# A decoder layer on one core: x and the first weights on one queue, cross attention in whole banks, w_co in turns with the heads, the last k-tiles of down block by block

## The chip, the core and the metric

The kernel runs on one core of a Trainium2 chip. The metric is device time in microseconds, from several executions; lower is better. One execution was also taken by the hardware profiler.

## What is computed

One decoder layer on a sequence of 256 tokens with a model width of 1024, in fp32, with 256 memory tokens for cross attention and a feed-forward width of 2816:

```python
x = x + 0.5 * swiglu(rms_norm(x, g_ffn1), w_ffn1_gu, w_ffn1_down)
h = rms_norm(x, g_mix); proj = h @ w_in            # q, k, v of 16 heads
x = x + concat(rms_norm(dilated attention, 12 heads), rms_norm(MoBA attention, 4 heads)) @ w_out
x = x + cross_attention(rms_norm(x, g_cross), rms_norm(mem, g_mem), w_cq, w_ckv, w_co)   # 4 heads of 256
x = x + 0.5 * swiglu(rms_norm(x, g_ffn2), w_ffn2_gu, w_ffn2_down)
return rms_norm(x, g_final)
```

Cross attention: q = h @ w_cq; k and v from mem @ w_ckv; scores times 1/16, softmax over the 256 memory tokens, times v, then @ w_co.

## The kernel before

Activations are kept transposed: `X[0..7]` are eight blocks of 128 features x 256 tokens. Every fp32 operand is split in two float32r parts, a high part and the rest (the low part), and a product is the sum of three: high x high, low x high, high x low. Weights are split by `wsplit` (ACT copies the high part, DVE subtracts for the low part: L125 and L126), activations by `split` (L313 and L314 without a gain, L316 and L317 with one). A split activation block lies as 256 columns of high and 256 columns of low part side by side.

Two ways to do the three products stand next to each other. `mmT_run` and `mm2` take one matmul with the high weights on all 512 columns and one with the low weights on the 256 high ones; the result is two halves of a 512-column PSUM bank, which `halves` or `add_halves` must add (an ACT copy, a DVE add) before anything else. `mm3` and `mmT_wide` take three matmuls of 256 columns into 256 columns of a bank; nothing has to be added. `mmT_wide` goes through all blocks with one operand before it takes the next. Each matmul has its weight load.

Weights come as chunks of 512 KB (two k-tiles x 512 columns) through four raw buffers, issued by SP (`wload`, L118), and are split into eight `w` buffers. `projT` is a projection of four blocks: `spread` takes all blocks k-tile by k-tile, `abreast` two blocks at a time, and the last `whole` blocks go as three products each. `downT` (first FFN only) and `addT` (w_out, w_co) add their result to X, and `block` then splits X for the next stage and adds its squares to the sum for the norm.

The order on TensorE is the program's; the other engines' order is set by the framework's planner, except in `start()`, where everything is in program order. To mix stages on TensorE the program keeps a clock by hand: every matmul helper calls `tick` with its estimated time, `later(d, f)` puts f on a list for d us on, and `tick` fires what is due. `until` fires events until something exists.

`start()` is the opening: x (1 MB in three pieces, by ACT's queue) and the first four weight chunks `w0(0)` to `w0(3)` (by SP's queue) are loaded, x is transposed by TensorE (`prepare(j)`, two blocks at a time), and the first gate projection runs k-tile by k-tile over four blocks with `mmT_wide` (L238). `WARM` = 5 matmuls on the identity run at the very start, two more between the first transposes and the first product (an fp32 matmul is two passes in the trace, so ten and four).

The cross stage: `cross_qp` makes q in two halves c (four blocks, two heads each); after each half its heads' `scores` are due by `later`, and each head's probabilities are transposed by `turn`, 5.0 behind its scores. `projT` emits all four blocks before the loop over them begins. `cross_o` makes a head's output from V and the transposed probabilities. In the w_co step, `addT` first takes k = 0 to 3 for all blocks, then calls `cross_o` for heads 2 and 3, then finishes block by block.

The mem load is in two halves (`half`), each transposed by `turn` some us behind on the hand-kept clock.

## Time and profile before

| | |
|---|---|
| time, median of 3 executions | 621.33 us (619.17 to 621.79) |
| profiled execution | 621.25 us |
| its span, first to last instruction | 619.5 us |
| TensorE busy | 601.9 us (97%) |
| VectorE (DVE) busy | 445.0 us (72%) |
| ScalarE (ACT) busy | 350.7 us (57%) |
| moved by DMA | 110.02 MB, mean 178 GB/s |

Busy time of TensorE is that of its matmuls, which are pipelined: a matmul's row lasts longer than the distance to the next one, so its speed is read from the spacing of starts. An idle time stands in brackets behind a row, with what ended it. PEld is the weight loads, L12 is line 12 of the program. The rows of the trace stand further down.

### The profile page before, as it was taken

Reading aid. Unit: us, or ns where it says so; the run is one execution under the profiler, and the core shown is the slowest. Engines: PE = TensorE matmul, PEld = TensorE weight load, DVE = VectorE, ACT = ScalarE, POOL = GpSimd, SP = SyncE. Lnnn points to the kernel's source line nnn. Section 1 sums busy time; section 2 is a strip of 40 time slices with the busy share of each in tenths; the row PEclk is TensorE's granted clock in tenths of the full one; section 3 lists DMA queues with packets and bytes.
Section 4 is the critical chain, followed back from the end, with each engine's and each line's share of the span. In section 5 each row is a group of like instructions: output and inputs, shape, how many; then the busy total and the mean of one; then the engine's idle time right before and its main releaser. Section 6 shows DMA issues by size and latency. Waiting matters only on the chain.

```text
span 619.5 us, 9485 instructions
## 1 busy us (share of the span) xinstructions
PE 601.9 (97%) x3488; PEld 519.4 (84%) x3488; DVE 445.0 (72%) x754; ACT 350.7 (57%) x614; POOL 57.0 (9%) x90
## 2 busy tenths in 40 slices
PE   7999999999999999999999998889999999999995
PEld 6998888888898887778878887778888888888885
DVE  3899747897475866774888886868788788794424
ACT  4766535665454665565675565756564565664312
POOL 0000110000010241222301120003000000000000
PEclk9999999999999999999999998999999999999999
DMA  7667997577666627444336644333646646476501
GB/s 238 227 213 245 208 243 231 181 236 252 213 188 191 199 88 237 137 137 137 122 116 204 234 138 140 105 99 112 230 149 224 204 153 222 170 242 201 167 1 68
DMA packets 58989, 110.02 MB, mean 178 GB/s; under 512 B 3760, under 2 KB 14608, under 8 KB 58944
## 3 DMA queue, kind: packets, MB, share of 16 engines
q1 hardware_dynamic: 56848, 104.44, 52.1%
q0 software_dynamic: 832, 2.88, 2.7%
q10 hardware_dynamic: 1264, 2.10, 0.9%
q8 instruction: 27, 0.44, 0.3%
q14 instruction: 18, 0.15, 0.1%
HBM read 107.58 MB, written 1.84 MB: 177 GB/s over the span
## 4 chain that ended last, share of the span: by engine, by line
PE 90%; DVE 4%; DMA 2%; ACT 2%; issue 1%; POOL 0%; ACTq 0%; POOLq 0%; SPq 0%
PE bank L224 41%; PE bank L228 20%; PE bank L188 7%; PE bank L189 7%; PE bank L190 7%; PE bank L238 3%; DVE w L126 2%; PE bank L490 1%; PE bank L537 1%; DMA slot<-in_x_dram 1%; PE bank L521 1%; DVE slot L317 1%; DMA slot<-in_mem_dram 1%; ACT w L125 1%; DMA raw<-in_w_co_dram 1%
## 5 line engine op out<-in xcount | busy, mean ns | idle before, releaser
L224 PE MATMUL bank<-slot,w 128*128 128x512 f32 x1162 | 364.4, 397 | 4.6 <-DVE slot L314 3.6
L126 DVE TENSOR_TENSOR w<-raw,w 128x1024 fp32r<-128x1024 f32 (+1 forms) x197 | 237.5, 1222 | 72.9 <-ACT w L125 72.3
L125 ACT ACTIVATE w<-raw 128x1024 fp32r<-128x1024 f32 (+1 forms) x197 | 201.9, 1051 | 96.1 <-PE bank L190 42.7
L228 PEld LDWEIGHTS bank<-slot,w 128*128 128x128 f32 x1162 | 214.6, 188 | 49.2 <-issue 1.5
L228 PE MATMUL bank<-slot,w 128*128 128x256 f32 x1162 | 228.2, 280 | 0.0
L224 PEld LDWEIGHTS bank<-slot,w 128*128 128x128 f32 x1162 | 180.0, 189 | 9.3 <-DVE slot L314 4.2
L270 ACT ACTIVATE hv<-bank 128x256 f32<-128x256 f32 x120 | 43.9, 376 | 36.0 <-PE bank L228 30.6
L188 PE MATMUL bank<-w,slot 128*128 128x512 f32 (+1 forms) x156 | 60.8, 390 | 0.0
L189 PE MATMUL bank<-w,slot 128*128 128x512 f32 (+1 forms) x156 | 60.0, 384 | 0.0
L190 PE MATMUL bank<-w,slot 128*128 128x512 f32 (+1 forms) x156 | 59.9, 384 | 0.0
L188 PEld LDWEIGHTS bank<-w,slot 128*128 128x128 f32 x156 | 29.3, 188 | 6.0 <-issue 0.5
L190 PEld LDWEIGHTS bank<-w,slot 128*128 128x128 f32 x156 | 29.3, 188 | 5.9
L189 PEld LDWEIGHTS bank<-w,slot 128*128 128x128 f32 x156 | 29.3, 188 | 5.5
L313 ACT ACTIVATE slot<-u 128x512 fp32r<-128x512 f32 x22 | 13.9, 630 | 31.6 <-DVE u L408 31.4
L335 POOL TENSOR_TENSOR ssq<-ssq,sq 128x256 f32<-128x256 f32 x28 | 24.3, 867 | 71.9 <-ACT sq L330 71.5
L317 DVE SCALAR_TENSOR_TENSOR slot<-X,gT,slot 128x256 fp32r<-128x256 f32 x30 | 19.9, 674 | 6.6 <-ACT slot L316 6.4
L271 DVE TENSOR_TENSOR u<-bank,hv 128x256 f32<-128x256 f32 x40 | 16.8, 421 | 9.7 <-ACT hv L270 9.6
L403 ACT ACTIVATE g<-g 128x512 f32<-128x512 f32 x22 | 13.7, 630 | 17.7 <-DVE g L285 17.7
L508 ACT ACTIVATE pt<-pt,nm 128x128 f32<-128x128 f32 (+1 forms) x32 | 14.2, 445 | 15.2 <-DVE nm L506 15.2
L271 DVE TENSOR_TENSOR g<-bank,hv 128x256 f32<-128x256 f32 x40 | 16.4, 421 | 8.6 <-ACT hv L270 8.4
L316 ACT ACTIVATE slot<-X,gT 128x256 fp32r<-128x256 f32 x30 | 14.8, 506 | 12.7 <-DVE X L296 12.7
L335 POOL TENSOR_TENSOR ssq<-sq 128x256 f32<-128x256 f32 x6 | 5.7, 945 | 172.6 <-ACT sq L330 172.6
(132 smaller groups left out, 523.1 us busy)
## 6 DMA issues: line engine op xcount, KB each, us to landing
raw<-in_w_ffn_gu_dram SPq DMA_DIRECT2D x88, 512.0 KB, 4.6
raw<-in_w_ffn_down_dram SPq DMA_DIRECT2D x44, 512.0 KB, 4.5
raw<-in_w_ckv_dram SPq DMA_DIRECT2D x16, 512.0 KB, 5.0
raw<-in_w_in_dram SPq DMA_DIRECT2D x12, 512.0 KB, 3.6
raw<-in_w_in_dram SPq DMA_DIRECT2D x24, 256.0 KB, 4.2
raw<-in_w_out_dram SPq DMA_DIRECT2D x8, 512.0 KB, 4.9
raw<-in_w_cq_dram SPq DMA_DIRECT2D x8, 512.0 KB, 5.1
raw<-in_w_co_dram SPq DMA_DIRECT2D x8, 512.0 KB, 3.8
```

The lines of the kernel that those rows point to most:

```text
L125: nc.scalar.activation(w[:, 0, a:b], raw[:, a:b], AF.Copy)
L126: nc.vector.tensor_tensor(w[:, 1, a:b], raw[:, a:b], w[:, 0, a:b].bitcast(F32), OP.subtract)
L188: nc.tensor.matmul(ps, ah, bh, start=start, stop=False)
L189: nc.tensor.matmul(ps, al, bh, start=False, stop=False)
L190: nc.tensor.matmul(ps, ah, bl, start=False, stop=stop)
L224: nc.tensor.matmul(ps, w[:, 0, o + blk * P:o + (blk + 1) * P], both(xs, k), start=k == first, stop=False)
L228: nc.tensor.matmul(ps[:, :256], w[:, 1, o + blk * P:o + (blk + 1) * P], both(xs, k)[:, :256], start=False, stop=k == last)
L238: nc.tensor.matmul(ps, w[:, wp_, o + blk * P:o + (blk + 1) * P], a, start=start and i == 0, stop=stop and i == 2)
L270: nc.scalar.activation(t, ps[:, 256:], AF.Copy)
L271: nc.vector.tensor_tensor(out, ps[:, :256], t, OP.add)
L317: nc.vector.scalar_tensor_tensor(l, src, g, h.bitcast(F32), OP.mult, OP.subtract)
L335: (eng or nc.gpsimd).tensor_tensor(new, self.ss, sq, OP.add)
```

## The change

Five places change. In `start()`, SP issues x too, in turns with w0: x's first 256 columns, w0(0), x's next 256, w0(1), x's last 512, w0(2), w0(3); and four instead of two identity matmuls run before the first product. In `downT` the last six k-tiles, instead of the last two, go block by block. The mem transposes are due 6.0 instead of 4.0 behind their load. In the cross stage, the first half of q goes through `mmT_wide` into 256 columns per block, the scores' delays change, and `cross_o` does one head per call with `mm3`, both parts in one bank. In w_co the steps alternate with heads 2 and 3: k = 0 for all blocks, k = 2 for two, head 2, k = 2 for the other two, head 3, then k = 4 and k = 6 for all.

```diff
     def load_x(c0, n):
         hf, o = divmod(c0, 512)
-        nc.scalar.dma_start(x0[hf].rearrange("p (a n) -> p a n", n=512)[:, :, o:o + n],
+        nc.sync.dma_start(x0[hf].rearrange("p (a n) -> p a n", n=512)[:, :, o:o + n],
                           x_in[0, :, c0:c0 + n].rearrange("(a p) n -> p a n", p=P))
...
     def projT(wk, xs, nblk, spread=False, whole=0, abreast=False):
         res = [bank() for _ in range(nblk)] if spread or abreast else []
+        if spread and whole:
+            res = [b[:, :256] for b in res]
+            for k in range(KT):
+                mmT_wide(res, wk, xs, k, k == 0, k == KT - 1)
+            return res
         if spread:
...
-            for k in range(0, FK - 2, 2):
+            for k in range(0, FK - 6, 2):
                 for blk in range(4):
                     step(k, blk)
             for blk in range(4):
-                step(FK - 2, blk)
+                for k in range(FK - 6, FK, 2):
+                    step(k, blk)
                 add_halves(X[c * 4 + blk], b[blk], 0.5)
                 block(c * 4 + blk)
 
-    def addT(wd, src, block, early=0, more=None):
+    def addT(wd, src, block, order=None):
         for c in range(2):
             wk = colchunk(wd, c * 512, 512)
-            if c == 0 and early:
+            if c == 0 and order:
                 b = [bank() for _ in range(4)]
-                for k in range(0, early, 2):
-                    for blk in range(4):
+                for step in order:
+                    if callable(step):
+                        step()
+                        continue
+                    k, blks = step
+                    for blk in blks:
                         mmT_run([(b[blk], k, blk), (b[blk], k + 1, blk)], wk, src, 0, KT - 1)
-                more()
-                for blk in range(4):
-                    for k in range(early, KT, 2):
-                        mmT_run([(b[blk], k, blk), (b[blk], k + 1, blk)], wk, src, 0, KT - 1)
-                    add_halves(X[blk], b[blk], 1.0)
-                    block(blk)
+                        if k == KT - 2:
+                            add_halves(X[blk], b[blk], 1.0)
+                            block(blk)
                 continue
...
-            later(4.0, turn, hf, m)
+            later(6.0, turn, hf, m)
...
-            for blk, ps in enumerate(projT(colchunk(w_cq, c * 512, 512), xs, 4, spread=(c == 0))):
+            for blk, ps in enumerate(projT(colchunk(w_cq, c * 512, 512), xs, 4, spread=(c == 0), whole=4 * (c == 0))):
...
-                    later(2.6 + 2.0 * (blk // 2) if c == 0 else 1.8, scores, c * 2 + blk // 2)
+                    later(3.0 + 3.0 * (blk // 2) * (c == 0), scores, c * 2 + blk // 2)
...
-    def cross_o(V, PT, OT, hs):
-        for h in hs:
-            until(lambda: PT[h] is not None)
-            t = work.tile([P, 512], F32, tag="g1", name="on", bufs=3)
-            for e in range(2):
-                et = (h % 2) * 2 + e
-                op = bank()
-                for i in range(2):
-                    vs = V[i][h // 2]
-                    mm2(op, vs[:, et * P:(et + 1) * P], vs[:, 512 + et * P:512 + (et + 1) * P],
-                        both(PT, h * 2 + i), i == 0, i == 1)
-                halves(t[:, e * 256:e * 256 + 256], op)
-            s = slot()
-            split(s, 0, 2, t)
-            OT.append(s)
+    def cross_o(V, PT, OT, h):
+        until(lambda: PT[h] is not None)
+        op = bank()
+        for e in range(2):
+            et = (h % 2) * 2 + e
+            for i in range(2):
+                vs = V[i][h // 2]
+                ph, pl = act(PT, h * 2 + i)
+                mm3(op[:, e * 256:e * 256 + 256], vs[:, et * P:(et + 1) * P],
+                    vs[:, 512 + et * P:512 + (et + 1) * P], ph, pl, i == 0, i == 1)
+        s = slot()
+        split(s, 0, 2, op)
+        OT.append(s)
...
     def start():
+        load_x(0, 256)
         nc.scalar.dma_start(grow[0:8], g_ffn1.rearrange("l (k p) -> (l k) p", p=P))
-        load_x(0, 256)
+        load_w0(0)
         load_x(256, 256)
+        load_w0(1)
         load_x(512, 512)
-        for i in range(4):
-            load_w0(i)
+        load_w0(2)
+        load_w0(3)
...
-        for i in range(2):
+        for i in range(WARM - 1):
             nc.tensor.matmul(gps[:, :P], ident, ident, start=True, stop=True)
...
-        cross_o(V, PT, OT, (0, 1))
+        cross_o(V, PT, OT, 0)
+        cross_o(V, PT, OT, 1)
         xs, st, block = next_x("ffn2")
-        addT(w_co, OT, block, 4, lambda: cross_o(V, PT, OT, (2, 3)))
+        every = range(4)
+        addT(w_co, OT, block, ((0, every), (2, (0, 1)), lambda: cross_o(V, PT, OT, 2), (2, (2, 3)),
+                               lambda: cross_o(V, PT, OT, 3), (4, every), (6, every)))
```

## Rows read from the trace of the kernel before

**Rows 1.** The page's busy times: busy us (share of the span) x instructions.

```profile
PE 601.9 (97%) x3488; PEld 519.4 (84%) x3488; DVE 445.0 (72%) x754; ACT 350.7 (57%) x614; POOL 57.0 (9%) x90
```

**Rows 2.** TensorE's matmuls in order of time, those with a wait ahead of them: start us, length us, line and operation, output <- inputs, [idle before <- what ended it].

```profile
7.28 1.12 PE L728 MATMUL bank<-ident,slot 128*128 128x128 f32 x4 [3.23 <-DMA slot<-in_x_dram]
...
208.42 1.20 PE L224 MATMUL bank<-slot,w 128*128 128x512 f32 x4 [0.75 <-DVE slot L317]
...
219.72 1.06 PE L566 MATMUL bank<-ident,slot 128*128 128x128 f32 x8 [0.42 <-DMA slot<-in_mem_dram]
...
375.15 0.39 PE L188 MATMUL bank<-slot 128*128 128x256 f32 x1 [0.36 <-ACT slot L313]
...
376.41 0.39 PE L189 MATMUL bank<-slot 128*128 128x256 f32 x1 [0.88 <-DVE slot L314]
...
402.31 0.50 PE L224 MATMUL bank<-slot,w 128*128 128x512 f32 x1 [1.92 <-DVE slot L314]
...
410.75 0.72 PE L224 MATMUL bank<-slot,w 128*128 128x512 f32 x2 [1.72 <-DVE slot L314]
```

**Rows 3.** The opening: instructions in order of time, and three pieces of the chain of waits (start us, length us, what).

```profile
3.78 0.27 PE L720 MATMUL bank<-ident,grow 8*128 8x8 f32 x1
...
8.19 1.06 PE L747 MATMUL bank<-ident 128*128 128x128 f32 x4
...
15.50 0.60 PE L728 MATMUL bank<-ident,slot 128*128 128x128 f32 x4
15.86 3.13 PE L238 MATMUL bank<-slot,w 128*128 128x256 f32 x24
...
21.42 3.90 ACT L125 ACTIVATE w<-raw 128x1024 fp32r<-128x1024 f32 x4
...
9.25 2.73 PE bank L238 x12
11.98 0.80 PE bank L728 x4
```

**Rows 4.** Transfers in the opening: the load of x's first piece in the chain of waits (issue ended at the start given, length to landing); bytes by queue up to 4.3 us (q1 is SP's queue, q10 ACT's; packets, MB, share of 16 engines); and four stretches (us from start, length, busy time of each engine, granted clock, DMA share, GB/s).

```profile
1.37 5.87 DMA slot<-in_x_dram
...
q1 hardware_dynamic: 364, 0.71, 54.0%
q10 hardware_dynamic: 17, 0.01, 0.5%
...
0.00:3.20 3.20, 1.85 (x8) 1.85 (x9) 0.17 (x2) 0.18 (x1) 0.68 (x6) 1.00 0.37 87
3.20:4.60 1.40, 0.85 (x5) 0.53 (x3) 0.17 (x1) 1.30 (x2) 0.00 (x0) 1.00 1.04 391
4.60:6.70 2.10, 0.00 (x0) 0.00 (x0) 0.00 (x0) 0.00 (x0) 0.00 (x0) 1.00 1.03 366
6.70:11.20 4.50, 3.92 (x18) 3.83 (x19) 2.17 (x4) 3.19 (x7) 0.00 (x0) 1.00 0.97 347
```

**Rows 5.** The end of down, in order of time: the first matmuls of the q projection, its sixth step, and the split of the seventh block.

```profile
199.09 1.09 PE L224 MATMUL bank<-slot,w 128*128 128x512 f32 x4
...
206.10 1.09 PE L224 MATMUL bank<-slot,w 128*128 128x512 f32 x4
...
207.41 0.95 DVE L317 SCALAR_TENSOR_TENSOR slot<-X,gT,slot 128x256 fp32r<-128x256 f32 x1
```

**Rows 6.** The second mem load in the chain of waits.

```profile
215.29 4.29 DMA slot<-in_mem_dram
```

**Rows 7.** The first cross scores: DVE's instructions in order of time, two stretches (columns as in rows 4, the granted clock third from the end), and the page's granted clock in 40 slices of 15.5 us.

```profile
374.23 0.42 DVE L271 TENSOR_TENSOR hq<-bank,hv 128x256 f32<-128x256 f32 x1
...
374.81 1.21 DVE L126 TENSOR_TENSOR w<-raw,w 128x1024 fp32r<-128x1024 f32 x1
...
375.94 0.42 DVE L314 TENSOR_TENSOR slot<-hq,slot 128x256 fp32r<-128x256 f32 x1
...
374.60:377.70 3.10, 1.52 (x7) 0.72 (x5) 2.89 (x10) 1.87 (x6) 0.00 (x0) 1.00 0.93 320
377.70:381.20 3.50, 3.50 (x15) 3.31 (x16) 2.33 (x8) 1.75 (x6) 0.00 (x0) 0.52 0.36 133
...
PEclk9999999999999999999999998999999999999999
```

**Rows 8.** The w_co step in order of time: the split of head 1's output, head 2's transposes and their split.

```profile
401.57 0.68 DVE L314 TENSOR_TENSOR slot<-on,slot 128x512 fp32r<-128x512 f32 x1
...
402.65 0.60 PE L658 MATMUL bank<-ident,cpt 128*128 128x128 f32 x4
...
403.28 0.60 ACT L313 ACTIVATE slot<-bank 128x512 fp32r<-128x512 f32 x1 [1.80 <-PE bank L658]
...
403.92 0.69 DVE L314 TENSOR_TENSOR slot<-bank,slot 128x512 fp32r<-128x512 f32 x1 [0.52 <-ACT slot L313]
```

**Rows 9.** Weight loads by line (count | busy us, mean ns of one | idle), and the time from issue to landing of the weight transfers in the first 40 us.

```profile
L228 PEld LDWEIGHTS bank<-slot,w 128*128 128x128 f32 x1162 | 214.6, 188 | 49.2 <-issue 1.5
L238 PEld LDWEIGHTS bank<-slot,w 128*128 128x128 f32 x144 | 18.9, 203 | 0.2
...
DMA to landing us min/median/max: 3.8/5.2/9.4
```

## The prediction

> **What bounds the kernel now.** I read the page's shares first: TensorE is busy 97% of the span [rows 1]. So only two things move the time: matmul work added or removed, and the places where TensorE waits. The order of its instructions is the program's own, so I next listed, in order of time, every place where it waited [rows 2]: for x at 7.28 us, at the end of the first down projection (208.42), for mem (219.72), at the first cross scores (375.15, 376.41), and twice in the first half of w_co (402.31 and 410.75). Besides waits, TensorE runs slowly in two stretches. At 377.7 to 381.2 the granted clock is 0.52 where it is 1.00 just before, nearly all of it at 1.2 instead of 2.4 GHz, right behind the waits at 375 and 376; it is the only one of the 40 slices that the page shows under nine tenths [rows 7]. In the opening the column for the granted clock reads 1.00 throughout [rows 4], but the spacing tells the same two levels: twelve 256-column matmuls from 9.25 take 2.73 us (0.23 each), twenty-four from 15.86 take 3.13 with the last one's tail (about 0.122 each) [rows 3]. Everything else on TensorE is one stream without gaps, so a stall taken out early stays out, unless a later one takes it back.
>
> **Opening.** The first transposes start at 7.28, when x's first 256 columns have landed; they were issued at 1.37 on ACT's queue [rows 2, 4]. Up to 4.3 us that queue moved 0.01 MB while SP's, with the weights, moved 0.71 [rows 4]. After the change x's first piece (262 KB) is the first on SP's queue. All queues together moved 87 GB/s x 3.2 us = 278 KB by 3.2 us, then 391 GB/s [rows 4]; so the piece is through by about 3.2 and landed by about 3.8, or 4.3 if its shorter 1 KB runs move more slowly at the start. TensorE is busy until 4.05 (gain transpose, 3.78 + 0.27) [rows 3]. Transposes therefore begin at 4.1 instead of 7.28. By the same running sum w0(0) (786 KB in all) is through at 4.5, x's second piece at 5.2, w0(1) at 6.7, x's last at 8.2, w0(2) and w0(3) at 9.7 and 11.2. With half a microsecond allowed for landing each is there before it is due: w0(3), the latest, was split before ACT began on the up half at 21.42 [rows 3], so not before 16 now.
>
> From transposes to the first real matmul it took 0.91 us and four matmul passes of warming, 8.19 to 9.25. Now there are four warming matmuls, each two passes: eight passes at 0.265 = 2.12, 1.06 more. Matmuls followed the warming without a wait before, when it was shorter, so ACT's and DVE's splits are in time and the first matmul is at 4.1 + 0.91 + 2.12 = 7.15. The twelve matmuls of k = 0 cost 2.73 at the low spacing or 12 x 0.122 = 1.46 at the high one, and the four transposes behind them 0.80 or 0.36 [rows 3]. I take the high one: the engine now works from 1.35 on with hardly a pause, where before it stood still 3.23 us ahead of the transposes and the spacing fell while it worked on. So matmuls of k = 1 start at 7.15 + 1.46 + 0.36 = 9.0 instead of 12.78: 3.8 earlier. Bounds: still the low spacing, 2.1; high spacing already in the warming passes, 4.8. I take 3.5. The transfers behind it are paced by the splits that free the four raw buffers, which move along.
>
> A rule speaks against this part: the Trainium skill ("DMA: Bandwidth & Descriptors", section "Issuing engines are not separate DMA queues") has transfers from several engines interleave on the same 16 DMA engines and lets the choice of the issuer save only issue time. Rows 4 disagree for the opening (0.01 MB against 0.71 by 4.3 us); by the rule the sum would lose nearly all of the 3.5 us.
>
> **End of the first down projection.** Now each block runs its last six k-tiles in one go: 3 steps of two pairs (a 512- and a 256-column matmul), 0.70 us each (half of a spread step's 1.40, below), so blocks end 2.1 us apart, not 0.7. The number of matmuls is the same. The wait at 208.42 is for the split of the seventh block (DVE 207.41 + 0.95), one of four add-and-split chains that pile up when down ends at 199.09 [rows 5]. With 2.1 us between blocks, blocks 4 to 6 end 6.3, 4.2 and 2.1 us before the last one, and its chain alone has ten until k = 7 is due. Price of the wait: from 199.09 to 206.10 are five spread steps, 1.40 each, so the step after 206.10 was due at 207.50 and came at 208.42: 0.9 back. Three weight buffers are held to the end, three weight splits (1.2 us of DVE each, as at 374.81 [rows 7]) come later, for weights of the k projection that are due 11 us on. Bounds 0.5 and 0.9; I take 0.9.
>
> **mem.** Its transposes fire 6 instead of 4 us after the load on the hand-kept clock. The second load landed 4.3 us behind its issue (215.29) and cost 0.42 of waiting [rows 2, 6]; 2 us more covers it. 0.4, at worst 0.
>
> **Cross queries.** The first half now goes as 8 x 12 matmuls of 256 columns at 0.122 = 11.7 us, for 8 steps of 1.40 = 11.2 (32 pairs of 512 and 256) [rows 3, 5]: 0.5 more. In exchange nothing has to be added from two bank halves: per block DVE has one step of 0.42 where it had two [rows 7], and ACT one where it had two. This chain is what the scores waited for: the halves were added on DVE at 374.23, a weight split of 1.21 came in at 374.81, and the low part of the first block was written at 375.94 [rows 7]. Cost of that: seven matmuls in 3.1 us (7 x 0.12 = 0.8): 2.3; and 3.5 us at clock 0.52: 1.7. Together 4.0. DVE turned to this chain at 374.23; with one step instead of two the first low part can be there at 374.7, the second at 375.2, or at 376.4 if the same weight split lies between. Scores, at 3.0 instead of 2.6 on the hand-kept clock, are due at 375.5 (374.6 before, 0.5 and 0.4 later). I leave 0.5 of waiting and no fall of the clock: waits of 1.92 and 1.72 at 402 and 410 did not bring it down [rows 2, 7]. Net 4.0 - 0.5 - 0.5 = 3.0; bounds -0.5 (all stays) and 3.5.
>
> **Cross outputs and w_co.** Per head 12 matmuls of 256 for 4 pairs: 4 x 0.36 for 4 x 0.35, nothing. Evacuation falls to one ACT and one DVE step, 0.60 and 0.69 as for the transposes at 402.65 [rows 8], from three on each. The wait at 402.31 is for head 1's output, written on DVE at 401.57 behind the softmax of heads 2 and 3, because scores had been pushed between its two parts. Now scores come behind head 1's matmuls (3.0 us against 2 x 4 x 0.33 = 2.64 on the hand-kept clock): 24 score matmuls and the first k-step, 2.9 + 2.8 us, lie ahead of its use, its chain takes 1.3 plus a weight split or two. 1.9 back. The wait at 410.75 is for heads 2 and 3 together. Now 2.8 us of other matmuls lie between each head and its use. 1.7 back.
>
> New is a wait that was covered. Scores of heads 2 and 3 fire at 3.1 on that clock; head 2's transposes are due 5.0 after its own, at 9.4, and by then only k = 0 and two blocks of k = 2 have gone: 9.48. So head 2's output follows its transposes at once. Before, transposes at 402.65 gave the high part at 403.88 and the low part at 404.61 [rows 8], with w_co steps in between. The first output matmul waits 1.23 - 0.48 = 0.75 and the third another 0.5: 1.3 lost; behind it w_co's steps and head 3 queue on TensorE. Bounds 0 (softmax and split earlier) and 2.5 (a weight split of 1.22 on DVE first). I take 1.3.
>
> **Sum.** 3.5 + 0.9 + 0.4 + 3.0 + 1.9 + 1.7 - 1.3 = 10.1 us. The profiled execution took 621.25 us (span 619.5 and 1.75 around it), as good as the median 621.33. 621.25 - 10.1 = 611.2. All lows together (2.1, 0.5, 0, -0.5, 3.6 for the two, -2.5) leave 3.2, all highs 13.2.
>
> **Rivals.** *DVE stays late in the cross stage.* The order on DVE is the planner's; if a weight split goes ahead of the query splits and of head 2's split, the scores wait as before and the new wait is 2.5: 3.5 + 0.9 + 0.4 - 0.5 + 3.6 - 2.5 = 5.4, 615.9. For it: the 1.21 us split at 374.81. Against: half of DVE's other work there is gone. 0.12.
> *The queue gives nothing.* x lands only as much earlier as it is issued earlier (0.73 for 1.37), so 0.64 - 1.06 for the extra passes = -0.4 instead of 3.5: 615.1. Against it rows 4. 0.11. (It is what the Trainium skill's rule on issuing engines, above, comes to.)
> *Weight loads set the pace.* The change makes 32 + 16 more of them; at 188 ns [rows 9] 9.0 us, for the 0.5 counted: 621.25 - 1.6 = 619.7, no change. Against: matmuls of 256 columns follow one another at 0.122 while their loads last 0.203 [rows 3, 9], in the opening, so loads overlap. 0.06. (The Trainium skill, "Perfetto Trace Analysis", section "Identifying the Most-Contended Engine", says that the busy share of weight loads is the measure of TensorE's headroom, not that of matmuls; here 84% [rows 1]. The spacing shows that this share can still rise.)
> *One queue serves one transfer at a time* (slower). At the least landing time of 3.8 us [rows 9] seven transfers end at 0.73 + 26.6 = 27.3 and the four chunks of the up half behind them at 42.5; the last of those was split at about 24.3 (21.42 + 3 x 0.97) [rows 3]. The opening would lose 18.2, the rest gains 6.6: 632.9. It decides once that chunk lands later than about 31. Against: SP's four weight loads already overlapped (0.71 MB by 4.3). 0.04.
> The forecast keeps 0.67, with an own range of 608 to 613.5.
>
> **How the numbers follow.** Executions shown spread from 619.17 to 621.79, so 0.5% (3 us) is about what can be told from no change. Faster: 0.67 + 0.12 + 0.11 = 0.90; same 0.06; slower 0.04. The range takes in the first two rivals and the upper bounds: 607.8 to 615.9 leaves out the other two and some tails.
>
> **What would show it.** x's transposes at about 4.1 and matmuls at 0.122 apart from about 7; x's and weights' pieces landing in turn. No wait of TensorE behind down. Score matmuls without gaps, granted clock 1.00 in the slice at 372 to 387. In w_co one wait of about 1.3 at the first output matmul behind head 2's transposes, none later. I am wrong if the opening still runs at 0.24 apart until 12, if a wait over 2 us appears behind those transposes, or if gaps appear in stages that the change does not touch.

## The result, and the profile after

The changed kernel takes 610.75 us (median of 4 executions, 610.66 to 610.81); the kernel before took 620.26 on the same chip (619.17 to 621.79). The ratio is 0.9845, 95% interval 0.9818 to 0.9872. The forecast was 611.2. The profiled execution took 610.66 us with a span of 608.9, against 621.25 and 619.5. The four executions of the kernel before lie in two pairs (619.17 and 619.19, 621.33 and 621.79) and the profiled one lies with the upper pair, so that the traces differ by 10.6 us and the medians by 9.5.

The page of the changed kernel, busy times and granted clock, to be held against [rows 1] and the last line of [rows 7]:

```profile
PE 598.6 (98%) x3540; PEld 519.4 (85%) x3540; DVE 440.6 (72%) x742; ACT 346.4 (57%) x602; POOL 59.9 (10%) x90
...
PEclk9999999999999999999999999999999999999999
```

There are 52 more matmul records, and TensorE is busy 3.3 us less: no slice is under nine tenths of the full clock any more. The waits are to be held against [rows 2]. These are TensorE's matmuls with a wait ahead of them, from its first product on, in order of time (start us, length us, line, output <- inputs, [idle before <- what ended it]):

```profile
6.49 1.70 PE L238 MATMUL bank<-slot,w 128*128 128x256 f32 x12 [0.31 <-ACT w L125]
...
386.10 0.73 PE L224 MATMUL bank<-slot,w 128*128 128x512 f32 x2 [1.00 <-DVE slot L319]
...
394.55 0.39 PE L188 MATMUL bank<-slot 128*128 128x256 f32 x1 [0.69 <-ACT slot L318]
...
395.50 0.39 PE L190 MATMUL bank<-slot 128*128 128x256 f32 x1 [0.45 <-DVE slot L319]
```

None of the waits of before is left at its place. Three new, smaller ones stand in the w_co stage, and one of 0.31 us stands in the opening. Where the time went is read by setting the same instruction of both traces side by side. The start of each in us, how much earlier it is, and what each stretch gave:

| instruction of TensorE | before | after | earlier by | stretch gave | forecast |
|---|---|---|---|---|---|
| third group of x transposes | 15.50 | 11.97 | 3.53 | opening 3.53 | 3.5 |
| first matmul of the q projection | 199.09 | 195.58 | 3.51 | 0.0 | 0 |
| first matmul of the k projection | 211.75 | 207.23 | 4.52 | end of down 1.01 | 0.9 |
| first matmul of the cross queries | 360.31 | 355.15 | 5.16 | mem and what is near it 0.64 | 0.4 |
| first matmul of head 0's output | 391.04 | 382.06 | 8.98 | queries, scores, clock 3.82 | 3.0 |
| first matmul of the second FFN | 427.66 | 416.85 | 10.81 | outputs and w_co 1.83 | 2.3 |
| last matmul | 612.87 | 602.29 | 10.58 | -0.23 | 0 |

The opening of the changed kernel in order of time, to be held against [rows 3]: TensorE's matmuls, then two of ACT's weight splits, its split of x's next two blocks, and the weight loads that wait for that:

```profile
3.98 1.11 PE L735 MATMUL bank<-ident,slot 128*128 128x128 f32 x4
4.89 1.30 PE L754 MATMUL bank<-ident 128*128 128x128 f32 x8
...
8.03 0.60 PE L735 MATMUL bank<-ident,slot 128*128 128x128 f32 x4
8.39 3.74 PE L238 MATMUL bank<-slot,w 128*128 128x256 f32 x24
11.97 0.60 PE L735 MATMUL bank<-ident,slot 128*128 128x128 f32 x4
...
5.81 0.63 ACT L125 ACTIVATE w<-raw 128x512 fp32r<-128x512 f32 x1 [0.63 <-DMA raw<-in_w_ffn_gu_dram]
...
8.15 1.06 ACT L125 ACTIVATE w<-raw 128x1024 fp32r<-128x1024 f32 x1 [0.17 <-DMA raw<-in_w_ffn_gu_dram]
...
9.65 0.91 ACT L321 ACTIVATE slot<-X,gT 128x256 fp32r<-128x256 f32 x2
...
10.21 0.53 PEld L238 LDWEIGHTS bank<-slot,w 128*128 128x128 f32 x4 [0.35 <-ACT slot L321]
```

Two stretches of it, to be held against the second and third of [rows 4] (us, busy times of the engines, granted clock, DMA share, GB/s):

```profile
3.20:4.60 1.40, 1.40 (x8) 1.15 (x7) 0.17 (x1) 0.00 (x0) 0.00 (x0) 1.00 0.93 318
4.60:6.70 2.10, 1.79 (x12) 1.60 (x11) 0.71 (x2) 1.37 (x3) 0.00 (x0) 1.00 0.95 292
```

x's transposes follow the gain's without a wait, at 3.98. The first product is no longer behind x but behind the first weights: ACT waits for w0(0) until 5.81 and for w0(1) until 8.15. Behind the split of w0(1) come the copy and the split of x's next two blocks, and the matmuls of k = 2 wait for these.

The next lines are the seventh step of the q projection, the second mem transposes, the split that the first scores read (DVE), and the first scores. None of the three on TensorE has an idle time in brackets, where before each of them waited:

```profile
204.00 1.09 PE L224 MATMUL bank<-slot,w 128*128 128x512 f32 x4
...
218.54 1.04 PE L573 MATMUL bank<-ident,slot 128*128 128x128 f32 x8
...
369.11 1.41 DVE L319 TENSOR_TENSOR slot<-bank,slot 128x256 fp32r<-128x256 f32 x4
...
370.13 0.28 PE L188 MATMUL bank<-slot 128*128 128x256 f32 x1
```

### The profile page after: what moved, and what is told of

Read it like the earlier page. It is cut to its first block, busy times and chain, and to the rows that moved or that the text cites. A ratio compares the mean times of both kernels' runs of the same rounds, so it can differ in the third digit from the quotient of the medians.

```text
span 608.9 us, 9549 instructions
## 1 busy us (share of the span) xinstructions
PE 598.6 (98%) x3540; PEld 519.4 (85%) x3540; DVE 440.6 (72%) x742; ACT 346.4 (57%) x602; POOL 59.9 (10%) x90
## 3 DMA queue, kind: packets, MB, share of 16 engines
HBM read 107.58 MB, written 1.84 MB: 180 GB/s over the span
## 4 chain that ended last, share of the span: by engine, by line
PE 95%; DVE 1%; DMA 1%; issue 1%; ACT 1%; SPq 0%; POOLq 0%; POOL 0%
PE bank L224 43%; PE bank L228 22%; PE bank L188 7%; PE bank L190 7%; PE bank L189 7%; PE bank L238 4%; PE bank L497 1%; PE bank L544 1%; DMA raw<-in_w_ffn_gu_dram 1%; PE bank L528 1%; ACT w L125 1%; DVE w L126 1%; PE bank L367 0%; DVE slot L319 0%; PE bank L352 0%
## 5 line engine op out<-in xcount | busy, mean ns | idle before, releaser
L224 PE MATMUL bank<-slot,w 128*128 128x512 f32 x1130 | 355.3, 396 | 1.0 <-DVE slot L319 1.0
L228 PEld LDWEIGHTS bank<-slot,w 128*128 128x128 f32 x1130 | 209.3, 188 | 48.5 <-issue 1.5
L228 PE MATMUL bank<-slot,w 128*128 128x256 f32 x1130 | 222.2, 279 | 0.0
L224 PEld LDWEIGHTS bank<-slot,w 128*128 128x128 f32 x1130 | 174.4, 189 | 4.4 <-issue 1.3
L275 ACT ACTIVATE hv<-bank 128x256 f32<-128x256 f32 x108 | 39.7, 377 | 31.3 <-PE bank L228 29.8
L340 POOL TENSOR_TENSOR ssq<-ssq,sq 128x256 f32<-128x256 f32 x28 | 26.1, 934 | 74.2 <-ACT sq L335 73.8
L238 PE MATMUL bank<-slot,w 128*128 128x256 f32 x240 | 31.2, 286 | 0.5 <-ACT w L125 0.3
L238 PEld LDWEIGHTS bank<-slot,w 128*128 128x128 f32 x240 | 29.4, 191 | 1.1 <-ACT w L125 0.5
```

The lines of the kernel that those rows point to most:

```text
L224: nc.tensor.matmul(ps, w[:, 0, o + blk * P:o + (blk + 1) * P], both(xs, k), start=k == first, stop=False)
L228: nc.tensor.matmul(ps[:, :256], w[:, 1, o + blk * P:o + (blk + 1) * P], both(xs, k)[:, :256], start=False, stop=k == last)
L238: nc.tensor.matmul(ps, w[:, wp_, o + blk * P:o + (blk + 1) * P], a, start=start and i == 0, stop=stop and i == 2)
L275: nc.scalar.activation(t, ps[:, 256:], AF.Copy)
L340: (eng or nc.gpsimd).tensor_tensor(new, self.ss, sq, OP.add)
```

## The experiments

All start from the changed kernel and change one thing, but for one run that joins two; "after" is its 610.75 us, and each ratio is against the kernel before on the same chip. The runs come from two chips, and the quickest executions of the kernel before are 0.5 us apart on these (619.13 and 618.66), so a difference to "after" of that size says little without its trace.

**The issue of x undone.** x goes by ACT's queue again, behind the gain row, and the weights by SP's; the four warming matmuls stay.

```diff
-        nc.sync.dma_start(x0[hf]...
+        nc.scalar.dma_start(x0[hf]...
...
-        load_x(0, 256)
         nc.scalar.dma_start(grow[0:8], ...
-        load_w0(0)
-        load_x(256, 256)
-        load_w0(1)
-        load_x(512, 512)
-        load_w0(2)
-        load_w0(3)
+        load_x(0, 256)
+        load_x(256, 256)
+        load_x(512, 512)
+        for i in range(4):
+            load_w0(i)
```

> The changed kernel with only the opening's loads put back: x by ACT's queue, the four weight chunks by SP's, in the old order; four warming matmuls stay. Theory (x's early landing is the gain): x's transposes start at about 7.3 us again, the first product waits for eight warming passes at the low spacing, and the kernel is 3.5 to 4.6 us slower than the changed one, 614.3 to 615.4 us. Rival (the queue does not matter, only the warming does): x lands 0.6 us later than in the changed kernel at most, under 1 us slower, below 611.8.

Measured: 613.89 us (613.46 to 614.61), ratio 0.9893 [0.9863, 0.9923]; 3.1 more than after, a little less than the theory's 3.5. TensorE in order of time:

```profile
7.28 1.12 PE L733 MATMUL bank<-ident,slot 128*128 128x128 f32 x4 [3.23 <-DMA slot<-in_x_dram]
8.19 1.92 PE L752 MATMUL bank<-ident 128*128 128x128 f32 x8
```

The wait of [rows 2] is back with its start and length to the hundredth. So this edit carries the opening's gain. It doesn't say yet whether the queue does it or the turn.

**Two warming matmuls instead of four.**

```diff
-        for i in range(WARM - 1):
+        for i in range(2):
```

> The changed kernel with two instead of four identity matmuls between x's first transposes and the first product. In the changed kernel the first product waits for ACT's split of the first weights, which waits for their landing (5.8 us), not for the warming. Theory A (the extra passes lie in that wait): same time within 0.3 us, the twelve products of k = 0 at the same spacing of about 0.13. Theory B (the extra passes are what keeps TensorE at the high level): those twelve at 0.2 or more and 0.8 to 1.5 us slower. Theory C (they cost their own time): 0.5 us faster.

Measured: 610.74 us median, ratio 0.9848 [0.9822, 0.9874], the same as after; but of its four executions (611.63, 610.63, 610.68, 610.80) the profiled one is the slowest:

```profile
4.90 1.06 PE L754 MATMUL bank<-ident 128*128 128x128 f32 x4
6.28 2.93 PE L238 MATMUL bank<-slot,w 128*128 128x256 f32 x12 [0.32 <-ACT w L125]
...
12.91 0.60 PE L735 MATMUL bank<-ident,slot 128*128 128x128 f32 x4
```

There the twelve matmuls of k = 0 ran at the low spacing (6.28 to 9.01, 0.23 each), and the third transposes came 0.94 later than after. The two extra matmuls cost nothing, since the product waits 0.3 us for w0(0) either way, and whether they buy anything depended on the execution: about 1 us in one of four. So the profiled execution fits theory B and the other three fit theory A's time. Why this one differs is not shown.

**Down's last two k-tiles block by block, as before, instead of six.**

```diff
-            for k in range(0, FK - 6, 2):
+            for k in range(0, FK - 2, 2):
...
-                for k in range(FK - 6, FK, 2):
+                for k in range(FK - 2, FK, 2):
```

> The changed kernel with down's last two instead of last six k-tiles block by block, as before. Theory: the wait of TensorE ahead of the seventh k-tile of the q projection comes back, 0.7 to 1.0 us slower, 611.4 to 611.8. Rival (that wait had another cause, such as a weight split in the way, and has gone with the shifted schedule): within 0.3 us.

Measured: 611.83 us (611.59 to 611.93), ratio 0.9862 [0.9837, 0.9887]; 1.1 more than after, of which some 0.2 is the opening of this execution (third group of x transposes at 12.16 for 11.97). The wait is back, in the place and of the size of [rows 2]:

```profile
205.08 1.20 PE L224 MATMUL bank<-slot,w 128*128 128x512 f32 x4 [0.76 <-DVE slot L322]
```

**The mem transposes due 4 us behind the load again.**

```diff
-            later(6.0, turn, hf, m)
+            later(4.0, turn, hf, m)
```

> The changed kernel with the mem transposes due 4.0 instead of 6.0 behind their load. Theory: the wait for the second mem load comes back, 0.4 to 0.6 us slower. Rival (the rest of the schedule has moved so far that the load is in time anyway): within 0.2 us.

Measured: 611.26 us (611.19 to 611.49), ratio 0.9849 [0.9831, 0.9867]; 0.5 more than after. The wait for mem is 0.84 here where it was 0.42 [rows 2]; the opening of this execution was 0.2 quicker (11.76 for 11.97), so the time does not show all of it:

```profile
215.38 1.06 PE L573 MATMUL bank<-ident,slot 128*128 128x128 f32 x8 [0.84 <-DMA slot<-in_mem_dram]
```

**Cross queries in halves again**, the new delays of the scores kept.

```diff
-  projT(colchunk(w_cq, c * 512, 512), xs, 4, spread=(c == 0), whole=4 * (c == 0))
+  projT(colchunk(w_cq, c * 512, 512), xs, 4, spread=(c == 0))
```

> The changed kernel with the first half of the cross queries in bank halves again (pairs of 512 and 256 columns, an ACT copy and a DVE add per block); the delays of the scores stay at 3.0 and 6.0. Theory (the chain from bank to split query is what the scores waited for): waits of TensorE of 1.5 to 2.5 us at the first scores, perhaps with the clock at 0.5 behind them, minus 0.3 us of matmuls: 1.2 to 3.8 us slower. Rival (the later scores alone cover it): 0.3 us faster to 0.3 slower.

Measured: 613.03 us (612.79 to 614.29), ratio 0.9886 [0.9859, 0.9913]; 2.3 more than after. Two of the old waits are back:

```profile
371.37 0.38 PE L189 MATMUL bank<-slot 128*128 128x256 f32 x1 [0.88 <-DVE slot L319]
372.15 0.39 PE L188 MATMUL bank<-slot 128*128 128x256 f32 x1 [0.28 <-ACT slot L318]
```

The first has the length that it had before [rows 2], and so has the second, which in the kernel before was

```profile
377.20 0.38 PE L188 MATMUL bank<-slot 128*128 128x256 f32 x1 [0.28 <-ACT slot L313]
```

But here the granted clock didn't fall behind them: it is 1.00 from 369 to 377 us. So of the 3.82 us of this stretch the halves alone cost 2.3. The fall to 0.52 [rows 7] did not come back in the profiled execution. One of the four executions, 614.29 us, has a mean granted clock of 0.994, the other three 0.997 to 0.999; it has no trace.

**Cross outputs in halves again**, the new order kept.

```diff
-        op = bank()
+        t = work.tile([P, 512], F32, tag="g1", name="on", bufs=3)
         for e in range(2):
             et = (h % 2) * 2 + e
+            op = bank()
             for i in range(2):
                 vs = V[i][h // 2]
-                ph, pl = act(PT, h * 2 + i)
-                mm3(op[:, e * 256:e * 256 + 256], ..., ph, pl, i == 0, i == 1)
+                mm2(op, ..., both(PT, h * 2 + i), i == 0, i == 1)
+            halves(t[:, e * 256:e * 256 + 256], op)
         s = slot()
-        split(s, 0, 2, op)
+        split(s, 0, 2, t)
```

> The changed kernel with the cross outputs as before: two banks per head, pairs of 512 and 256 columns, halves added by ACT and DVE, then the split; the order of the w_co steps stays. Theory (the shorter way out of the bank matters wherever a head's output is used soon): the wait for head 0's output, 1.0 us in the changed kernel, grows by 0.8 to 1.5, the later heads stay covered by 2.8 us of other matmuls: 0.8 to 2 us slower. Rival (the order alone took the waits away): within 0.3 us.

Measured: 617.75 us (616.90 to 618.68, 10 executions), ratio 0.9955 [0.9939, 0.9972]; 7.0 more than after, far above what was expected. TensorE's waits in order of time:

```profile
389.06 1.19 PE L224 MATMUL bank<-slot,w 128*128 128x512 f32 x2 [4.06 <-DVE slot L319]
...
400.58 0.50 PE L205 MATMUL bank<-slot 128*128 128x512 f32 x1 [1.41 <-DVE slot L319]
...
407.11 0.73 PE L224 MATMUL bank<-slot,w 128*128 128x512 f32 x2 [1.62 <-DVE slot L319]
```

Two stretches behind the first of them (columns as above):

```profile
388.00:392.00 4.00, 2.94 (x12) 2.78 (x13) 3.04 (x5) 0.82 (x2) 0.00 (x0) 0.50 0.59 172
392.00:396.00 4.00, 4.00 (x23) 3.88 (x23) 2.59 (x13) 2.14 (x7) 0.00 (x0) 0.70 0.24 88
```

DVE ahead of it, in order of time, and below it the split of the same head's output in the changed kernel:

```profile
383.50 1.22 DVE L126 TENSOR_TENSOR w<-raw,w 128x1024 fp32r<-128x1024 f32 x1
...
385.30 1.22 DVE L126 TENSOR_TENSOR w<-raw,w 128x1024 fp32r<-128x1024 f32 x1
...
386.77 1.41 DVE L276 TENSOR_TENSOR on<-bank,hv 128x256 f32<-128x256 f32 x4
388.22 0.69 DVE L319 TENSOR_TENSOR slot<-on,slot 128x512 fp32r<-128x512 f32 x1
```

```profile
385.36 0.69 DVE L319 TENSOR_TENSOR slot<-bank,slot 128x512 fp32r<-128x512 f32 x1
```

Head 0's output matmuls are done before 384, but DVE has two weight splits and the second queries ahead of it, comes to the four adds at 386.77 and to the low part at 388.22. In the changed kernel that low part is written at 385.36, ahead of the second of these weight splits (386.47 there). Behind the wait of 4.06 us the granted clock is 0.50 (1.2 GHz), and the score matmuls from 390.04 to 394.31 run 0.213 apart instead of 0.12. Waits: 4.06 + 1.41 + 1.62 = 7.09 against 2.14 after, 4.95 more. Clock: the twenty steps between these two starts take 4.27 instead of some 2.4, 1.9 more, and the first k-step beside them 0.4. That is 7.2, the difference of the spans (616.1 and 608.9). The step that failed in the expectation: it counted the added work on ACT and DVE, but not what else would go ahead of it on DVE, nor the clock behind a long wait.

**Heads 2 and 3 together behind all of k = 2.**

```diff
-  ((0, every), (2, (0, 1)), <head 2>, (2, (2, 3)), <head 3>, (4, every), (6, every))
+  ((0, every), (2, every), <head 2>, <head 3>, (4, every), (6, every))
```

> The changed kernel with k = 0 and k = 2 of w_co for all blocks ahead of heads 2 and 3, which follow one another; then k = 4 and k = 6 for all. Theory: the wait at head 2's first output matmul (1.25 us in the changed kernel) is covered by the two blocks of k = 2 (1.4 us) and goes; head 2's output is used 1.4 us behind its matmuls, its chain takes about 1.6, so up to 0.5 us comes back there: 0.6 to 1.2 us faster, 609.5 to 610.1. Rival (alternating is what keeps head 2's output in time): a wait of 1 us or more at k = 4, same time or slower.

Measured: 609.59 us (609.34 to 609.77), ratio 0.9820 [0.9784, 0.9856]; 1.2 less than after. No wait is left at head 2's output, and one of 0.15 us appears where k = 4 starts:

```profile
399.02 0.74 PE L224 MATMUL bank<-slot,w 128*128 128x512 f32 x2 [0.15 <-DVE slot L319]
```

**The second scores due at 2.5 instead of 3.0** on the hand-kept clock, so that they go ahead of the first k-step of w_co.

```diff
-  later(3.0 + 3.0 * (blk // 2) * (c == 0), scores, ...)
+  later(3.0 + 3.0 * (blk // 2) if c == 0 else 2.5, scores, ...)
```

> The changed kernel with the scores of heads 2 and 3 due 2.5 instead of 3.0 us behind the second half of the queries, that is right behind head 1's output matmuls and ahead of the first w_co matmul. Theory: the wait of 1.0 us for head 0's output is covered by 2.9 us of score matmuls and goes; nothing else moves: 0.8 to 1.1 us faster, 609.6 to 610.0. Rival (the scores then wait for the last queries' split instead): a wait of 0.5 us or more at the first score matmul, gain under 0.5.

Measured: 609.49 us (609.20 to 609.52), ratio 0.9819 [0.9788, 0.9849]; 1.3 less than after. The wait of 1.00 us for head 0's output is gone; those at head 2 stay and add up to 1.20 (1.14 after). The gain is a little above the 0.8 to 1.1 expected:

```profile
392.82 0.39 PE L188 MATMUL bank<-slot 128*128 128x256 f32 x1 [0.22 <-ACT slot L318]
394.31 0.39 PE L190 MATMUL bank<-slot 128*128 128x256 f32 x1 [0.98 <-DVE slot L319]
```

**Both of these.**

> Both together: scores of heads 2 and 3 right behind head 1's matmuls, and heads 2 and 3 behind all of k = 2. If the two waits are independent the gains add: 1.4 to 2.3 us faster than the changed kernel, 608.4 to 609.3. If the softmax of head 2 is what is late, the second gain is smaller: 609.5 to 610.

Measured: 608.24 us (607.91 to 608.57), ratio 0.980 [0.9769, 0.983]; 2.5 less than after, the sum of the two single gains and 0.2 more than the most that was expected; it is the fastest kernel of this study. In its trace the first wait of TensorE, 1.35 us at its very start, is the only one left.

**All of x ahead of all weights**, on SP's queue.

```diff
         load_x(0, 256)
         nc.scalar.dma_start(grow[0:8], ...
-        load_w0(0)
         load_x(256, 256)
-        load_w0(1)
         load_x(512, 512)
+        load_w0(0)
+        load_w0(1)
         load_w0(2)
         load_w0(3)
```

> The changed kernel with all three pieces of x ahead of all four weight chunks on SP's queue, instead of in turns. In the changed kernel ACT waits for w0(0), landed at 5.8 us, and w0(1), landed at 8.1, so the opening goes at the pace of the transfers. Theory: w0(0) has 786 KB more ahead of it at about 0.35 MB per us, so the first product starts 2.2 us later, at about 8.7, and the chunk w0(1), which had all but x's last piece ahead of it already, lands 1.5 us later: 1.5 to 2.2 us slower, 612.2 to 613. Rival (TensorE's warm-up sets the pace): within 0.5 us.

Measured: 616.34 us (614.58 to 617.39), ratio 0.9927 [0.9901, 0.9952]; 5.6 more than after, 3.9 in the profiled execution, the fastest of the four. ACT's first weight split and TensorE's first product:

```profile
8.86 0.63 ACT L125 ACTIVATE w<-raw 128x512 fp32r<-128x512 f32 x1 [3.68 <-DMA raw<-in_w_ffn_gu_dram]
...
9.54 2.93 PE L238 MATMUL bank<-slot,w 128*128 128x256 f32 x12 [3.06 <-ACT w L125]
```

The expectation was 1.5 to 2.2. w0(0) now lands 3.0 us later, and behind the wait of 3.06 us the granted clock is 0.50 from 9.5 to 12.5 us, which the expectation did not price. So the turns are part of the gain: x's first piece must be first, and w0(0) second. The three executions without a trace have a mean granted clock of 0.993 and 0.994 for 0.995 in the profiled one, so the clock was low for longer in them; where is open.

**Only x's first piece by ACT**, as the first transfer of its queue, the gain row behind it.

```diff
-        nc.sync.dma_start(x0[hf]...
+        (nc.scalar if c0 == 0 else nc.sync).dma_start(x0[hf]...
```

> The changed kernel with x's first piece alone issued by ACT, as the first thing there, and the rest in turns by SP. It tells whether ACT's queue as such is served late, or whether x was late before because four weight chunks had been put on SP's queue first. Theory (what is queued first is served first, whichever queue): x's first piece lands at 4 to 4.6 us, w0(0) by 5.8: within 0.5 us of the changed kernel. Rival (ACT's queue is served behind SP's): it lands at 6 us or later and the kernel is 1 to 3 us slower. By the Trainium skill's page DMA: Bandwidth & Descriptors, section Issuing engines are not separate DMA queues, the two interleave: the theory's time.

Measured: 613.04 us (612.63 to 613.48), ratio 0.9878 [0.9856, 0.9900]; 2.3 more than after. TensorE's gain transpose in order of time:

```profile
5.46 0.27 PE L727 MATMUL bank<-ident,grow 8*128 8x8 f32 x1 [1.61 <-DMA grow<-in_g_ffn_dram]
```

The bytes by queue up to 3.2 us (q1 is SP's, q10 ACT's; packets, MB, share of 16 engines):

```profile
q1 hardware_dynamic: 91, 0.19, 36.8%
q10 hardware_dynamic: 12, 0.01, 1.1%
```

What waits here is the gain row, behind x on ACT's queue, so the run doesn't answer its question for x. The bytes ask another: both queues issued their first transfer at 0.73, SP's issue ended 0.06 us sooner, and by 3.2 us SP's weights had moved 0.19 MB and ACT's x 0.01:

```profile
0.73 0.44 SPq L708 DMA_DIRECT2D raw<-in_w_ffn_gu_dram  x1
0.73 0.50 ACTq L63 DMA_DIRECT2D slot<-in_x_dram  x1
```

Whether these 0.06 us or the queue decided that, this run can't tell.

**The same with the gain row by SP**, ahead of w0(0). Now w0(0) is issued at 1.18, 0.45 us behind x.

```diff
-        nc.scalar.dma_start(grow[0:8], ...
+        nc.sync.dma_start(grow[0:8], ...
```

> The changed kernel, but x's first 256 columns are issued by ACT (the first transfer of its queue, at 0.73) and the gain row by SP, ahead of w0(0); the rest as it is. So nothing but x can be late for x's transposes. Theory (ACT's queue is itself slow to start beside a busy SP queue: where x was first on ACT's queue with the gain row behind it, that queue had moved 0.01 MB by 3.2 us and SP's 0.19): x lands at 5.2 to 5.5, transposes wait from about 4.1 until then, and the time is 1.5 to 2.5 above the changed kernel's: 612.2 to 613.3. Rival (only what is queued second on ACT is late; x itself, issued at 0.73, lands by 4.3 as on SP): transposes at 3.9 to 4.3, 610.5 to 611.2.

Measured: 610.54 us (610.43 to 610.69), ratio 0.9835 [0.9818, 0.9853]; as fast as after. The theory fell, and the rival's time and its start of the transposes hold; its reason, that only what is second on ACT's queue is late, leaves out the 0.01 MB of x in the run before this one. TensorE in order of time, the two issues, then the bytes by queue up to 3.2 us:

```profile
3.98 1.11 PE L735 MATMUL bank<-ident,slot 128*128 128x128 f32 x4
...
11.96 0.60 PE L735 MATMUL bank<-ident,slot 128*128 128x128 f32 x4
```

```profile
0.73 0.43 ACTq L63 DMA_DIRECT2D slot<-in_x_dram  x1
...
1.18 0.41 SPq L708 DMA_DIRECT2D raw<-in_w_ffn_gu_dram  x1
```

```profile
q10 hardware_dynamic: 269, 0.26, 25.1%
q1 hardware_dynamic: 35, 0.04, 13.6%
```

x's transposes are at 3.98 and the third group at 11.96, as after, though x goes by ACT. This time ACT's queue had moved all of x's first piece by 3.2 us and SP's 0.04 MB. Not the queue made x late before, but its place in the order of issue over both queues: it was issued at 1.37, behind the weights that SP had begun to issue at 0.73.

## Why the prediction was right, and where it wasn't

The sum was 10.1 us and the trace gave 10.6 (621.25 - 610.66); the medians gave 9.5. Term by term:

**Opening, 3.5 against 3.53: right by two errors that cancel, and with one wrong reason.** x's transposes came at 3.98 (forecast 4.1). The eight passes of warming were put at 2.12 and took 1.60 to the first product, its wait of 0.31 in that, so they ran above the low spacing and k = 1 began at 8.39 instead of 9.0. (The sum for the first product is 7.13, not 7.15; and the 12.78 that 9.0 was held against is the end of a piece of the chain, while in order of time those matmuls of before start at 12.48, so the working gives 3.5 and not 3.8.) In return the twenty-four matmuls from 8.39 took until 11.97, 3.58 us, where at 0.122 they take 2.9: in the middle of them the weight loads of k = 2 wait 0.35 us for ACT's split of x's next blocks, which stands behind the late split of w0(1). The step that failed is the landing of the weights: by the running sum with the rates of [rows 4], w0(0) and w0(1) were to be there at 5.0 and 7.2, and ACT got them at 5.81 and 8.15. Lower rates are a part of it: 318 and 292 GB/s in the two stretches that had shown 391 and 366, with which the same running sum gives 5.2 and 7.7. The rest is the half microsecond allowed for landing: when w0(0) and w0(1) landed, 1.09 and 1.94 MB had moved in all, for the 0.79 and 1.57 of the sum, so 0.30 and 0.37 MB of transfers issued later had gone by, about 1 us of them at these rates. Whether x's shorter runs, now among the weights, lower the rate was only argued. The wrong reason: the low count of ACT's queue in [rows 4] was read as a slow queue, and with it the Trainium skill's rule ("DMA: Bandwidth & Descriptors", section "Issuing engines are not separate DMA queues") as contradicted. The last run agrees with that rule in that the issuer didn't matter: by ACT or by SP, 610.54 and 610.75. Of the interleaving that the section also names there is little in the bytes up to 3.2 us (0.26 against 0.04 MB). What the prediction took from the rule, that then hardly anything was to be gained, does not follow: the edit also moved x ahead of the weights in the order of issue, and that place is worth the 3.1 us of the first experiment.

**End of down, 0.9 against 1.01**, and 1.1 when undone: the step holds, wait, releaser and size.

**mem, 0.4 against 0.64**, and 0.5 when undone. The mechanism holds. The wait priced was that of before; with 4.0 in the quicker kernel it is 0.84.

**Cross queries, 3.0 against 3.82.** The chain behind the first queries was done before the scores, none of the 0.5 us of waiting stayed, and the clock stood at full. The 1.7 us counted for the clock is won only against executions of the kernel before that have the fall, as the profiled one has: of 33 that were taken beside the experiments, 23 have a mean granted clock of 0.994 or 0.995 and a median of 621.2 us, and ten have 0.997 or 0.998 and a median of 619.2. The wide form costs 11.96 - 11.65 = 0.31 us (355.15 to 367.11, the first matmul of the second half, against 360.31 to 371.96), where 0.5 was counted.

**Outputs and w_co, 2.3 against 1.83.** The two large waits went (1.92 + 1.72, and one of 0.23 at 397.37 that the prediction didn't list). The new wait at head 2 was put at 0.75 + 0.5 and measured 0.69 + 0.45, at the very matmuls named. The step that failed: head 0. Behind head 1's twelve matmuls come first the 512-column matmuls of one k-step (386.10) and only then the scores (386.67), since the hand-kept clock reads 2.64 there and the scores are due at 3.0; that step reads head 0's output, which only head 1's matmuls covered. The prediction followed head 1's output and missed this 1.00 us. Two of the experiments show both waits to be a matter of order and each worth about its own length.

**The rivals.** DVE late in the cross stage: not at the scores, but DVE ends two of the three waits that are left, and in the run with outputs in halves it is all of this rival and more. The queue that gives nothing fell with x's transposes at 3.98. Weight loads as the bound: there are 52 more of them, and the queries' stage, with most of these, grew by 0.31. The Trainium skill ("Perfetto Trace Analysis", section "Identifying the Most-Contended Engine") names the busy share of weight loads, beside the share of peak arithmetic (MFU), as the measure of TensorE's headroom; it went from 84% to 85% while the kernel became 1.6% faster, so 84% was not the wall here. One transfer at a time: w0(1), the fourth transfer, was there at 8.15.

Undone one by one, the parts cost 3.1, 1.1, 0.5, 2.3 and 7.0, more than the whole change gave: the new order with outputs in halves is far worse than both. The new order undone alone, with whole banks kept, was not tried.

## What to carry to other kernels

List the waits of the engine that is full, price each by its own length, and follow for each removed wait the next reader of the same buffer: the miss in w_co was a consumer one step nearer than the one looked at. Before moving a transfer to another queue, look at when it is issued against the large transfers of all queues; being first was worth 3.1 us here, the queue nothing. A step that shortens an evacuation (the way of a result out of its PSUM bank) on an engine with weight splits in its order can be worth more than its own work: here 7.0 us, where the adds that it spares take some 2.8 (an estimate: eight adds, of which four took 1.41).

## What had not been expected of the hardware

- Two queues side by side did not share evenly in the opening: the one whose first large transfer was issued first had nearly all bytes up to 3.2 us, SP's 0.19 MB against 0.01 with 0.06 us of lead, ACT's 0.26 against 0.04 with 0.45 us.
- TensorE's spacing rose at different moments behind the same work. With x by ACT and the gain row by SP the transposes began at 3.98 as after, but the twelve matmuls of k = 0 took 1.84 us (6.46 to 8.30) where they took 1.54 after (6.49 to 8.03); with two warming matmuls one execution of four was about 1 us longer. The granted clock reads 1.00 in the traced ones of these stretches whatever the spacing.
- The granted clock fell to 0.50 behind a wait of 4.06 us and behind one of 3.06. Behind waits of 0.36, 0.88 and 0.28 it was 0.52 in the kernel before [rows 7], and it stayed at 1.00 in the run with the last two of these. So short waits can go with a fall or without one, and within one kernel it differs by execution: the mean granted clock of the kernel before is 0.994 or 0.995 in 23 of 33 executions and 0.997 or 0.998 in ten.
